# HGRN and modulation in counted steps between the projections, and an earlier load in the FFN

## The chip, the cores and the metric

The kernel runs on one core of a Trainium2 chip. The metric is the device time of one execution in microseconds (us); lower is better. The engines carry the names of the profile: PE (TensorE), DVE (VectorE), ACT (ScalarE), POOL (GpSimd), and SP, which here only issues DMAs. PEld is PE's weight load.

## The reference

One decoder block, sequence 2048, model width 1024, float32. An input projection feeds two mixers, whose outputs are joined by an output projection; a SwiGLU FFN follows.

```
mod = silu(c) @ w_ada + b_ada                     # six vectors of 1024: shift, scale, gate, twice
h   = rms_norm(x, g1) * (1 + scale1) + shift1
hq, hf, hi, hg, aq, ak, av = split(h @ w_in)      # seven slices of 512 columns
# HGRN, 4 heads of 128: gated linear recurrence
state = exp(b_last) * state + (k * exp(b_last - b))^T v
o     = (q * exp(b)) state + (q k^T decayed, causal) v
hgrn  = rms_norm(o) * silu(hg)
# attention, 8 heads of 64: three dilated windows, joined by their softmax denominators
x = x + gate1 * ([hgrn, rms_norm(att)] @ w_out)
h = rms_norm(x, g2) * (1 + scale2) + shift2
x = x + gate2 * ((silu(h @ w_g) * (h @ w_u)) @ w_d)
out = rms_norm(x, final_g)
```

## The kernel before

Products of weights are made in three matmuls: each operand is split into a high and a low part (`whi`, `wlo`, `hhi`, `hlo`), and the product of the two low parts is left out. The sequence lies in four chunks of 512 positions, two to a half. A projection tile is 128x512 in a bank `psA`: eight steps over the model width, three matmuls each (lines 426 to 428 with the weights as columns, 527 to 529 with h). The 28 such tiles of each chunk make 28 x 4 x 24 = 2688 projection matmuls; the text counts the program by them ("the 1253rd").

While they run, the HGRN mixer is computed a head and a chunk at a time (`hg_mix`, 16 units). A unit has preparation (exponentials on ACT, the scan `hb` on DVE), four transposes to `psM` (L576), then seven levels: POOL and ACT make the decay `hd`, DVE makes the operand `hz` (two multiplications), PE makes four 128x128 products in the one bank `psL` (L604), and DVE copies the part under a mask into `hsc` (L609). Then come for each of four blocks the output `psO` (L618, L619), the state's update `psM` (L624) with its read `hst` on DVE (L627, L629), at the end a norm (`ss`, L636) and the store to `hg_d`. float32 matmuls run as two passes, so a level is eight entries of PE in the trace.

The modulation vectors that are needed late (32 of 48 columns of 128) are made in 16 pairs: two weight blocks `adaw` of 512 KB are loaded, DVE multiplies and adds them in eight steps (`adaacc`, L104, L106), two small matmuls sum over partitions (`psM`, L109), and `mods` is written. `x_stats` makes the norm of a chunk (L397), `make_h` the two parts of h (`hhi`, `hlo`).

The program is written in stages (`hg_half`, `token_major`, `att_qk`), and a scheduler moves instructions on every engine by its estimate of when their operands are there. At run time each engine then takes its own queue strictly in that order. Behind the last HGRN units stand the maxima of attention head 0 (L136: products of `qs` and `kh`, loaded back from `qk_d` in DRAM), and `combine` (L150): it transposes the maxima, sends them through DRAM (`m_d`, `mr`), joins the branches (`mm`, `mh`) and writes them back (`mn_d`), from where `qx` takes a row for attention's first scores (L797).

In the FFN's first pass `norm_out` ends the chunk before (sums of squares `ssq`, a matmul `nps` at L297, DVE and ACT apply it), `hr` holds raw blocks of the normalised h, loaded from `h2_d` (L917), and `operand_pieces` splits them into `chi` and `clo` for the first gate and up products `psG` (L904 to L906).

Of the kernel before, what the change touches and what calls it, by code (L numbers as in the profile page):

```python
# [10 lines left out]
F32 = mybir.dt.float32  # L11
# [38 lines left out]
def hybrid_block(ctx, tc, xT, small, cst, w_ada, w_ft, w_tk, w_out, w_gu, w_dn, out):  # L50
# [61 lines left out]

    def ada_pair(pl, pp, cact, g, bufs):
        ps = ada_sums(pl, cact, (g, g + 1), bufs, lambda: pp.tile([P, CH], F32, name="psM", tag="psM", bufs=1))
        tt(dve, mods[:, g:g + 2], ps[:, 0:2], sm[:, V_B + g:V_B + g + 2], ALU.add)
# [204 lines left out]
    def mix_tile(name):  # L320
        return cpool["mr"].tile([P, CH], F32, name="a" + name, tag="a" + name)
# [19 lines left out]
    with ExitStack() as ab:  # L341
# [44 lines left out]
        def x_stats(c, xs=None):  # L386
            ssq = xp.tile([P, CH], F32, name="ssq", tag="ssq", bufs=1)
            for k in range(KT):
                xk = xs[k] if xs else load_xk(c, k)
# [6 lines left out]
            ps = pp.tile([P, CH], F32, name="psM", tag="psM", bufs=1)  # L396
# [23 lines left out]

        def token_major_k(c, k, ps, whi, wlo):
            hhi, hlo = h_of[c]
            cs_ = slice((k % 2) * 512, (k % 2 + 1) * 512)
            for n in range(4):
                ts = slice(n * P, (n + 1) * P)
                pe.matmul(ps[n], hhi[:, k, ts], whi[:, cs_], start=k == 0, stop=False)
                pe.matmul(ps[n], hhi[:, k, ts], wlo[:, cs_], start=False, stop=False)
                pe.matmul(ps[n], hlo[:, k, ts], whi[:, cs_], start=False, stop=k == 7)

        with tc.tile_pool(name="ada0", bufs=2) as pl:  # L430
# [9 lines left out]
            def psum():  # L440
                tag = next(tags)
                return pp.tile([P, CH], F32, name=tag, tag=tag, bufs=1)
# [75 lines left out]
        def feature_major(half, ts, evac):  # L518

            ws_of = [split_w(wp, w_ft[t]) for t in ts]  # L520
            for c, i in [(c, i) for c in (2 * half, 2 * half + 1) for i in range(len(ts))]:
                whi, wlo = ws_of[i]
                hhi, hlo = h_of[c]
                ps = pp.tile([P, CH], F32, name="psA", tag="psA", bufs=4)
                for k in range(KT):
                    ws = slice(k * P, (k + 1) * P)
                    pe.matmul(ps, whi[:, ws], hhi[:, k, :], start=k == 0, stop=False)  # L527
                    pe.matmul(ps, whi[:, ws], hlo[:, k, :], start=False, stop=False)  # L528
                    pe.matmul(ps, wlo[:, ws], hhi[:, k, :], start=False, stop=k == 7)  # L529
                evac(ts[i], c, ps)  # L530

        def att_qk(half, pr):
# [5 lines left out]
            feature_major(half, (12 + pr, 16 + pr), evac)  # L538

        def hg_project(half, hd, js=(0, 1, 2), xs=None):  # L540
            xs = xs or {c: hw.tile([P, 3, CH], F32, name="hx", tag="hx", bufs=3) for c in (2 * half, 2 * half + 1)}

            def evac(t, c, ps):
                dve.tensor_scalar(xs[c][:, t // 4, :], ps, -43.0, None, ALU.max)
# [7 lines left out]
        def hg_mix(hd, c, x):  # L552
# [21 lines left out]
            kt_ps = pp.tile([P, CH], F32, name="psM", tag="psM", bufs=1)  # L574
# [13 lines left out]
            tt(dve, v2(zk)[:, :, 1], v2(kk)[:, :, 1], v2(lr)[:, :, 1], ALU.mult)  # L588
            for lv in range(7):
                h = 1 << lv  # L590
                if lv:
                    zk = zq = T("hz", 2)
                    dd = T("hd", 2)
                    w = lambda t: t.rearrange("p (n two h) -> p n two h", two=2, h=h)
                    ref = w(b)[:, :, 0, h - 1:h].broadcast_to([P, CH // (2 * h), h])
                    tt(pool, w(dd)[:, :, 0, :], ref, w(b)[:, :, 0, :], ALU.subtract)
                    tt(pool, w(dd)[:, :, 1, :], w(b)[:, :, 1, :], ref, ALU.subtract)
                    act.activation(dd, dd, AF.Exp)
                    tt(dve, w(zk)[:, :, 0, :], w(dd)[:, :, 0, :], w(kk)[:, :, 0, :], ALU.mult)
                    tt(dve, w(zk)[:, :, 1, :], w(dd)[:, :, 1, :], w(q)[:, :, 1, :], ALU.mult)  # L600
# [9 lines left out]

            tt(dve, q, q, eb, ALU.mult)
            o_ps = pp.tile([P, CH], F32, name="psO", tag="psO", bufs=1)
            v = v_of[c]
            for n in range(4):
                ts = slice(n * P, (n + 1) * P)
                vn = v[:, n, hd * P:(hd + 1) * P]
                if states[hd] is not None:
                    pe.matmul(o_ps[:, ts], states[hd], q[:, ts], start=n == 0, stop=False, skip_group_check=True)  # L618
                pe.matmul(o_ps[:, ts], vn, sc[:, ts], start=n == 0 and states[hd] is None, stop=n == 3,  # L619
                          skip_group_check=True)  # L620
                if c == NCH - 1 and n == 3:
                    break
                u = pp.tile([P, CH], F32, name="psM", tag="psM", bufs=1)
                pe.matmul(u[:, 0:P], kt[:, ts], vn, start=True, stop=True)  # L624
                new = hw.tile([P, P], F32, name="hst", tag=f"hst{hd}", bufs=2)
                if states[hd] is None:
                    dve.tensor_copy(new, u[:, 0:P])  # L627
                else:
                    dve.scalar_tensor_tensor(new, states[hd], eb[:, n * P + 127:n * P + 128], u[:, 0:P],  # L629
                                             ALU.mult, ALU.add)  # L630
                states[hd] = new
# [3 lines left out]
            ss = pp.tile([P, CH], F32, name="psM", tag="psM", bufs=1)  # L635
# [3 lines left out]
            y = T("hy", 2)  # L639
# [4 lines left out]
        def hg_half(half):  # L644
            first = None
            if half == 0:
                token_major(0, 0, (0,))
                first = hg_project(0, 0, (0, 1))
                token_major(0, 0, (1,))
            else:  # L650
                token_major(half, 0)
            prev = None
            for hd in range(HG_HEADS):
                xs = hg_project(half, hd, (2,), first) if first and hd == 0 else hg_project(half, hd)
                if prev:
                    for c, x in prev[1].items():
                        hg_mix(prev[0], c, x)
                prev = hd, xs
            return prev

        def first_maxima():

            tags = itertools.cycle(("psL", "psO", "psM"))

            def psum():
                tag = next(tags)
                return pp.tile([P, CH], F32, name=tag, tag=tag, bufs=1)
# [3 lines left out]
            for _ in maxima(0, psum):  # L671
                pass
            combine(0, psum)

        for half in range(2):
            if half:
                make_h(2)
            make_h(2 * half + 1)
            last = hg_half(half)
            token_major(half, 1)  # L680
            for pr in range(4):
                att_qk(half, pr)
                if pr == 0:
                    for c, x in last[1].items():
                        hg_mix(last[0], c, x)
                if half and pr == 1:
                    first_maxima()
                if half == 0 and pr == 1:
                    x_stats(2)
                    x_stats(3)  # L690
                if half == 0:
                    for g in range(16 + 8 * pr, 24 + 8 * pr, 2):
                        ada_pair(wp, pp, cact, g, 1)
# [3 lines left out]
    with ax:  # L697
# [135 lines left out]
        def finish_head(hd, c):  # L833
# [4 lines left out]
            rl = ap.tile([64, CH], F32, name="rl", tag="rl", bufs=4)  # L838
# [123 lines left out]
    with ExitStack() as wl, ExitStack() as w0:  # L962
# [3 lines left out]
        for nm in ("hg1", "at1"):  # L966
            c_pool(nm, wl)
# [19 lines left out]
        def norm_out(c, x, ssq, load=False):  # L987
# [36 lines left out]
        for i, (c, j) in enumerate(order):  # L1024
# [32 lines left out]
            if c + 1 < NCH:  # L1057
                if j == 3:
                    xs[c + 1] = load_xw(c + 1)
                if j == 4:  # L1060
# [3 lines left out]
                    last_part = att_half(ats[c + 1], raws, rstd)  # L1064
            if c == NCH - 1:
                if j == 0:
                    wr.close()
                    w0.close()
                    c_pool("hr", wl)
                    c_pool("hp", side="right")  # L1070
                    n = BLK[0][1]
                    tiles = [cpool["hr"].tile([P, KT, T], F32, name="hr", tag=f"hr{b}") for b in range(2)]
                    pieces = operand_pieces(h, [load_block(t, h2_d, b) for b, t in enumerate(tiles)], n,
                                            lambda n: w_tile("hv")[:, 0:n])
# [7 lines left out]
    with cx:  # L1082
# [14 lines left out]
        pace = []  # L1097

        def gate_up(f, h, n, wait=False, first=None):
# [38 lines left out]
            product(p5, parts(b22), h["S4"], start=False)  # L1138
# [66 lines left out]
        for p in range(3):  # L1205
# [103 lines left out]
```

## Time and profile before

| | |
|---|---|
| median of 3 runs | 3038.97 us (3032.05 to 3039.95) |
| profiled execution | 3040.49 us, span 3038.7 us, mean granted clock 0.982 |
| busy | PE 94%, PEld 85%, DVE 68%, POOL 46%, ACT 43% |
| to 107 us | first modulation and norm, first 198 projection matmuls |
| 107 to 978 | the other 2490 projection matmuls, HGRN, late modulation, first maxima |
| 978 to 1362 | attention |
| 1362 to 1575 | output projection |
| 1575 to 1655 | first part of the FFN |
| 1655 to 3039 | the rest of the FFN |

A busy share counts a matmul from its start to its end although the next one starts before that; the distance of starts is what a matmul costs. Idle time of PE is put down to the engine that released it.

### The profile page before, as it was taken

Reading aid. Unit: us, or ns where it says so; the run is one execution under the profiler, and the core shown is the slowest. Engines: PE = TensorE matmul, PEld = TensorE weight load, DVE = VectorE, ACT = ScalarE, POOL = GpSimd, SP = SyncE. Lnnn points to the kernel's source line nnn. Section 1 sums busy time; section 2 is a strip of 40 time slices with the busy share of each in tenths; the row PEclk is TensorE's granted clock in tenths of the full one; section 3 lists DMA queues with packets and bytes.
Section 4 is the critical chain, followed back from the end, with each engine's and each line's share of the span. In section 5 each row is a group of like instructions: output and inputs, shape, how many; then the busy total and the mean of one; then the engine's idle time right before and its main releaser. Section 6 shows DMA issues by size and latency. Waiting matters only on the chain. (4 is left out here: it accounts for less than half of the span.)

```text
span 3038.7 us, 45120 instructions
## 1 busy us (share of the span) xinstructions
PE 2847.3 (94%) x16308; PEld 2592.1 (85%) x16308; DVE 2063.4 (68%) x3781; ACT 1314.0 (43%) x2390; POOL 1411.9 (46%) x1074
## 2 busy tenths in 40 slices
PE   5899998888999999999988999999999999999998
PEld 4777776677778999998768999998999998999997
DVE  7566557667743665677767666679676669776676
ACT  3534423233532566566654333345343335443334
POOL 5344532244532323230035665665666656665664
PEclk9999999999999999999989999999999999999999
DMA  6311237411137756537754222222342223232222
GB/s 239 125 35 36 99 126 236 142 46 35 60 135 188 176 134 140 121 101 244 258 179 155 80 76 64 83 78 91 98 128 81 77 64 106 84 104 74 77 76 68
DMA packets 212031, 343.32 MB, mean 113 GB/s; under 512 B 24784, under 2 KB 97360, under 8 KB 208720
## 3 DMA queue, kind: packets, MB, share of 16 engines
q1 hardware_dynamic: 201984, 322.35, 34.7%
q10 hardware_dynamic: 9824, 18.09, 1.7%
q8 instruction: 128, 2.10, 0.3%
q14 instruction: 95, 0.78, 0.1%
HBM read 281.39 MB, written 58.98 MB: 112 GB/s over the span
## 5 line engine op out<-in xcount | busy, mean ns | idle before, releaser
L79 POOL TENSOR_TENSOR wlo<-wraw,whi 128x512 fp32r<-128x512 f32 (+1 forms) x540 | 845.4, 1586 | 729.5 <-ACT whi L277 384.3
L904 PE MATMUL psG<-chi,whi 128*128 128x344 f32 (+1 forms) x1848 | 597.5, 323 | 20.3 <-DVE hm L79 18.4
L906 PE MATMUL psG<-chi,wlo 128*128 128x344 f32 (+1 forms) x1848 | 593.1, 321 | 2.7 <-POOL wlo L79 2.6
L905 PE MATMUL psG<-clo,whi 128*128 128x344 f32 (+1 forms) x1848 | 594.8, 322 | 0.0
L277 ACT CAST whi<-wraw 128x512 fp32r<-128x512 f32 x520 | 311.7, 618 | 416.6 <-issue 188.8
L904 PEld LDWEIGHTS psG<-chi,whi 128*128 128x128 f32 x1848 | 351.6, 190 | 27.1 <-issue 10.5
L1166 PE MATMUL psD<-ahi,whi 128*128 128x344 f32 (+1 forms) x1056 | 345.5, 327 | 16.3 <-DVE xc L1169 15.8
L906 PEld LDWEIGHTS psG<-chi,wlo 128*128 128x128 f32 x1848 | 350.6, 190 | 3.7 <-POOL wlo L79 3.7
L1169 DVE SCALAR_TENSOR_TENSOR xc<-psD,mods,xc 128x344 f32<-128x344 f32 (+1 forms) x528 | 290.4, 568 | 90.0 <-PE psD L1168 89.7
L905 PEld LDWEIGHTS psG<-clo,whi 128*128 128x128 f32 x1848 | 350.4, 190 | 0.1
L79 POOL TENSOR_TENSOR wlo<-wt,whi 128x512 fp32r<-128x512 f32 x132 | 193.2, 1473 | 313.3 <-ACT whi L277 235.1
L1168 PE MATMUL psD<-ahi,wlo 128*128 128x344 f32 (+1 forms) x1056 | 336.9, 319 | 0.0
L1167 PE MATMUL psD<-alo,whi 128*128 128x344 f32 (+1 forms) x1056 | 335.9, 318 | 0.0
L79 DVE TENSOR_TENSOR hm<-hm,psG 128x344 f32<-128x344 f32 (+1 forms) x330 | 165.9, 503 | 239.3 <-PE psG L906 238.4
L527 PE MATMUL psA<-hhi,whi 128*128 128x512 f32 x640 | 261.1, 409 | 2.6 <-ACT hhi L412 2.6
L528 PE MATMUL psA<-hlo,whi 128*128 128x512 f32 x640 | 259.2, 405 | 0.2 <-DVE hlo L79 0.2
L529 PE MATMUL psA<-hhi,wlo 128*128 128x512 f32 x640 | 258.7, 405 | 0.0
L1166 PEld LDWEIGHTS psD<-ahi,whi 128*128 128x128 f32 x1056 | 198.7, 188 | 32.0 <-DVE xc L1169 27.8
L79 POOL TENSOR_TENSOR hd<-hb 128x256 f32<-128x256 f32 x192 | 134.0, 722 | 164.5 <-DVE hy L640 81.1
L1167 PEld LDWEIGHTS psD<-alo,whi 128*128 128x128 f32 x1056 | 198.8, 188 | 0.5
L1168 PEld LDWEIGHTS psD<-ahi,wlo 128*128 128x128 f32 x1056 | 198.6, 188 | 0.0
L277 ACT CAST whi<-wt 128x512 fp32r<-128x512 f32 x132 | 81.4, 617 | 234.4 <-DVE wt L79 140.1
(239 smaller groups left out, 6030.0 us busy)
## 6 DMA issues: line engine op xcount, KB each, us to landing
wraw<-in_w_gu SPq DMA_DIRECT2D x264, 256.0 KB
wraw<-in_w_dn SPq DMA_DIRECT2D x132, 256.0 KB
adaw<-in_w_ada SPq DMA_DIRECT2D x48, 512.0 KB
wraw<-in_w_ft SPq DMA_DIRECT2D x40, 512.0 KB
wraw<-in_w_tk SPq DMA_DIRECT2D x32, 512.0 KB
qk_d<-st SPq DMA_DIRECT2D x64, 256.0 KB
v<-v_d SPq DMA_DIRECT2D x16, 1024.0 KB
wraw<-in_w_out SPq DMA_DIRECT2D x64, 256.0 KB
```

The lines of the kernel that those rows point to most:

```text
L79: return eng.tensor_tensor(o, a, b, op)
L277: copy(hi, raw)
L527: pe.matmul(ps, whi[:, ws], hhi[:, k, :], start=k == 0, stop=False)
L528: pe.matmul(ps, whi[:, ws], hlo[:, k, :], start=False, stop=False)
L529: pe.matmul(ps, wlo[:, ws], hhi[:, k, :], start=False, stop=k == 7)
L904: pe.matmul(ps, w[0][:, ws], hi, start=start and k == 0, stop=False, skip_group_check=True)
L905: pe.matmul(ps, w[0][:, ws], lo, start=False, stop=False, skip_group_check=True)
L906: last = pe.matmul(ps, w[1][:, ws], hi, start=False, stop=stop and k == 3, skip_group_check=True)
L1166: pe.matmul(ps, w[z][0][:, ws], ahi, start=z == 0, stop=False)
L1167: pe.matmul(ps, w[z][0][:, ws], alo, start=False, stop=False)
L1168: pe.matmul(ps, w[z][1][:, ws], ahi, start=False, stop=z == 1)
L1169: dve.scalar_tensor_tensor(x, ps, ga2[:, j:j + 1], x, ALU.mult, ALU.add)
```

## The change

HGRN's unit, a modulation pair and `x_stats` become Python generators that yield between steps, and PE's order in the projection stage is the order in which the program is written (`manual_schedule`). A class `Beside` is told of every third projection matmul (`tick`) and takes the next step when its count is reached. In the first half two such queues run: the units of the head before, spread over 240 matmuls (its own 144 and the 96 of an attention pair), and the 16 pairs and two norms, spread over 1100. A level's operands are made two levels ahead; the state's four updates stand together ahead of the levels, in one bank, with `psM` in two buffers instead of one. In the second half the third and fourth heads' units are spread over token-major tiles and attention pairs alike. The maxima move from the last tile but one to the last tile's end, and `combine` behind it.

In the FFN the blocks `hr` are loaded a chunk sooner, into a pool of their own, the apply step of `norm_out` works in place, and its last part is released by the end of the first pass's first gate and up product. In attention `rl` has three buffers instead of four.

```diff
+        class Beside:
...
+            def begin(self, work, matmuls, steps, credit=0):
+                self.finish()
+                self.left.extend(work)
+                self.cost, self.credit = matmuls / steps, credit
+            def tick(self, n):
+                self.credit += n
+                while self.left and self.credit >= self.cost:
+                    self.credit -= self.cost
+                    self.step()
...
+            u = pp.tile([P, CH], F32, name="psM", tag="psM", bufs=2)
+            for n in ns:
...
+                pe.matmul(u[:, ts], kt[:, ts], vn[n], start=n == 0, stop=n == ns[-1], skip_group_check=True)
...
             for lv in range(7):
+                yield
+                zk, zq = zs.pop(lv)
...
+                if lv < 5:
+                    level(lv + 2)
...
+        def ada_steps(g):
+            w = wp.tile([P, 2, 8, P], F32, name="adaw", tag="adaw", bufs=1)
...
+            yield
+            yield
...
+            beside_ada.begin([ada_steps(g) for g in range(16, 48, 2)] + [x_stats_steps(2), x_stats_steps(3)],
+                             1100, 16 * 6 + 2 * 6)
+            for hd in range(1, HG_HEADS):
+                beside.begin(units(hd - 1, xs), 240, 2 * UNIT + 1)
+                xs = hg_project(0, hd)
+                att_qk(0, hd - 1)
+            beside.begin(units(3, xs), 288, 2 * UNIT + 1)
...
+            beside.begin(units(3, xs), 192, 2 * UNIT + 1)
+            att_qk(1, 1)
+            att_qk(1, 2)
+            beside.finish()
...
+            beside.begin([maxima(0, psum)], 96 - 36, 24, -36)
+        with tc.manual_schedule(engines={mybir.EngineType.PE}):
+            make_h(1)
+            first_half()
+            make_h(2)
+            make_h(3)
+            second_half()
+            first_maxima()
+            att_qk(1, 3)
+            beside.finish()
+        combine(0, first_psum[0])
...
-                v = w_tile("hv")
-                tt(dve, v, x[:, k, :], rstd, ALU.mult)
+                v = x[:, k, :]
+                tt(dve, v, v, rstd, ALU.mult)
...
+            if (c, j) == (2, 3):
+                blocks = [load_block(cpool["hr"].tile([P, KT, T], F32, name="hr", tag=f"hr{b}"), h2_d, b)
+                          for b in range(2)]
...
-                    steps = norm_out(NCH - 1, xs_last, boxes[NCH - 1]["ssq"], True)
+                    with tc.issue_after(ended[0]):
+                        steps = norm_out(NCH - 1, xs_last, boxes[NCH - 1]["ssq"], True)
```

PE in the first half, at the first HGRN unit, before: `psL` is a level, L624 a state's update, `psA` a projection.

```order
L604 MATMUL psL<-hzq,hz 128x128 x4
L527 MATMUL psA<-hhi,whi 128x512
L624 MATMUL psM<-vtok,hkt 128x128
L528 MATMUL psA<-hlo,whi 128x512
L529 MATMUL psA<-hhi,wlo 128x512
L604 MATMUL psL<-hz 128x128 x4
L624 MATMUL psM<-vtok,hkt 128x128
L527 MATMUL psA<-hhi,whi 128x512
L528 MATMUL psA<-hlo,whi 128x512
L529 MATMUL psA<-hhi,wlo 128x512
L604 MATMUL psL<-hz 128x128 x4
```

The same place now; L657 is the updates' line, L677 the levels', L732 a modulation pair's.

```order
L657 MATMUL psM<-vtok,hkt 128x128 x4
L565 MATMUL psA<-hhi,whi 128x512
L566 MATMUL psA<-hlo,whi 128x512
L567 MATMUL psA<-hhi,wlo 128x512
L732 MATMUL psM<-ones,adaacc 128x1 x2
L565 MATMUL psA<-hhi,whi 128x512
L566 MATMUL psA<-hlo,whi 128x512
L567 MATMUL psA<-hhi,wlo 128x512
L677 MATMUL psL<-hzq,hz 128x128 x4
L565 MATMUL psA<-hhi,whi 128x512
```

Levels stood three to six projection matmuls apart and now stand six to nine apart; the four updates are one group ahead of them, and modulation pairs, which stood between the 1253rd and the 1727th projection matmul for 12 of 16, come about every 60th from the 255th to the 1170th.

PE at the end of the projections before: L136 are the maxima of head 0, L150 is `combine`.

```order
L136 MATMUL psO<-kh,qs 128x128 x2
L136 MATMUL psM<-kh,qs 128x128 x2
L529 MATMUL psA<-hhi,wlo 128x512
L527 MATMUL psA<-hhi,whi 128x512
L528 MATMUL psA<-hlo,whi 128x512
L529 MATMUL psA<-hhi,wlo 128x512
L527 MATMUL psA<-hhi,whi 128x512
L150 MATMUL psL<-idt,mc 128x128
L528 MATMUL psA<-hlo,whi 128x512
L529 MATMUL psA<-hhi,wlo 128x512
```

The same place now; L133 are the maxima (`psS` those of head 1), L147 is `combine`, L896 attention's first scores.

```order
L565 MATMUL psA<-hhi,whi 128x512
L566 MATMUL psA<-hlo,whi 128x512
L567 MATMUL psA<-hhi,wlo 128x512
L133 MATMUL psM<-kh,qs 128x128 x4
L147 MATMUL psL<-idt,mc 128x128
L896 MATMUL psT<-qs,kh 128x256 x3
L133 MATMUL psS<-kh,qs 128x128
L133 MATMUL psS<-kh,qs 128x256 x15
L133 MATMUL psS<-kh,qs 128x128
```

Behind L150 stood 71 projection matmuls. Behind L147 stands none: the last is the row ahead of the last maximum, and head 1's maxima follow.

## Rows read from the trace of the kernel before

**Rows 1.** Busy time by stretch: us, PE, PEld, DVE, ACT, POOL (entries), clock, DMA share, GB/s

```profile
107.00:503.00 396.00, 366.53 (x1859) 291.94 (x1858) 237.43 (x397) 153.52 (x211) 157.00 (x142) 1.00 0.30 100
503.00:614.00 111.00, 95.98 (x398) 75.44 (x397) 77.64 (x120) 36.53 (x43) 31.90 (x14) 0.94 0.51 174
...
1575.00:1655.00 80.00, 59.18 (x322) 54.99 (x323) 60.53 (x76) 40.64 (x72) 58.83 (x40) 0.87 0.49 154
```

**Rows 2.** The same of the whole projection stage

```profile
107.00:978.00 871.00, 799.54 (x3971) 637.84 (x3969) 526.78 (x935) 317.70 (x432) 334.82 (x296) 0.98 0.32 104
```

**Rows 3.** PE's costliest groups, 107 to 978 us: busy, mean ns, idle before and releasers

```profile
L527 PE MATMUL psA<-hhi,whi 128*128 128x512 f32 x608 | 248.3, 408 | 0.0
...
L604 PE MATMUL psL<-hz 128*128 128x128 f32 x768 | 110.0, 287 | 29.1 <-DVE hsc L609 25.4 <-DVE hz L79 3.1
L426 PE MATMUL psA<-whi,hhi 128*128 128x512 f32 x222 | 91.0, 411 | 8.9 <-ACT hhi L412 4.3 <-DVE st L79 3.0 <-DVE hx L544 1.6
...
L109 PE MATMUL psM<-ones,adaacc 128*128 128x1 f32 x64 | 9.2, 248 | 19.2 <-DVE adaacc L106 19.2
```

**Rows 4.** PE in order of time at full clock: start, us, instruction

```profile
229.99 0.39 PE L527 MATMUL psA<-hhi,whi 128*128 128x512 f32 x1
...
230.67 0.39 PE L527 MATMUL psA<-hhi,whi 128*128 128x512 f32 x1
```

**Rows 5.** PE in order of time around four levels: [idle before <-releaser]

```profile
206.81 1.16 PE L604 MATMUL psL<-hz 128*128 128x128 f32 x8
207.72 0.47 PE L528 MATMUL psA<-hlo,whi 128*128 128x512 f32 x1
...
208.74 0.39 PE L529 MATMUL psA<-hhi,wlo 128*128 128x512 f32 x1
211.62 1.16 PE L604 MATMUL psL<-hz 128*128 128x128 f32 x8 [2.49 <-DVE hsc L609]
```

**Rows 6.** DVE's costliest groups, 107 to 978 us

```profile
L79 DVE TENSOR_TENSOR hz<-hd,hk 128x256 f32<-128x256 f32 x96 | 79.4, 827 | 7.4 <-ACT hd L598 6.8
L609 DVE COPY_PREDICATED hsc<-cs,psL 128x512 f32<-128x512 uint32 x96 | 69.7, 726 | 14.9 <-PE psL L604 14.3
L106 DVE SCALAR_TENSOR_TENSOR adaacc<-adaw,cact,adaacc 128x256 f32<-128x256 f32 x101 | 63.7, 631 | 2.3
L79 DVE TENSOR_TENSOR hz<-hd,hq 128x256 f32<-128x256 f32 x96 | 57.3, 597 | 0.0
L544 DVE TENSOR_SCALAR hx<-psA 128x512 f32<-128x512 f32 x45 | 30.9, 687 | 77.5 <-PE psA L529 77.4
```

**Rows 7.** DVE in order of time, the same stretch as rows 5

```profile
206.64 1.81 DVE L79 TENSOR_TENSOR hz<-hd,hk 128x256 f32<-128x256 f32 x1
...
212.27 0.41 DVE L79 TENSOR_TENSOR hz<-hd,hq 128x256 f32<-128x256 f32 x1
```

**Rows 8.** POOL in order of time, the same stretch

```profile
205.60 2.57 POOL L79 TENSOR_TENSOR wlo<-wraw,whi 128x1024 fp32r<-128x1024 f32 x1
```

**Rows 9.** DVE's waits, 450 to 645 us: us in total, times, longest

```profile
DVE adaacc L104 <- DMA adaw<-in_w_ada: 12.2, 7, 4.8
```

**Rows 10.** PE in order of time around the maxima of heads 0 and 1

```profile
943.56 0.39 PE L136 MATMUL psL<-kh,qs 128*128 128x128 f32 x2
...
961.39 0.27 PE L150 MATMUL psL<-idt,mc 128*128 128x128 f32 x1
...
985.56 1.52 PE L136 MATMUL psS<-kh,qs 128*128 128x128 f32 x6 [2.69 <-DMA kh<-qk_d]
```

**Rows 11.** SP's DMA issues around combine

```profile
928.14 0.53 SPq L216 DMA_DIRECT2D qs<-qk_d  x1
...
971.67 0.56 SPq L248 DMA_DIRECT2D qx<-mn_d  x2
```

**Rows 12.** PE's waits, 1575 to 1655 us

```profile
PE nps L297 <- DVE ssq L79: 9.6, 1, 9.6
PE psG L904 <- DVE hm L79: 8.1, 6, 3.9
```

More of the change, by code (lines that the diff above doesn't have):

```diff
@@ L1 @@
 import itertools
+from collections import deque
 from contextlib import ExitStack, nullcontext
@@ L419, in make_h, with __init__, step, finish @@
                 h_apply(c, k)
+        class Beside:
+            def __init__(self):
+                self.left, self.cost, self.credit = deque(), 1, 0
+            def step(self):
+                try:
+                    next(self.left[0])
+                except StopIteration:
+                    self.left.popleft()
+            def begin(self, work, matmuls, steps, credit=0):
[7 more added lines that the diff above has]
+                    self.step()
+            def finish(self):
+                while self.left:
+                    self.step()
+        beside, beside_ada = Beside(), Beside()
+        def tick(n=3):
+            beside.tick(n)
+            beside_ada.tick(n)
         def token_major_k(c, k, ps, whi, wlo):
@@ L516, in token_major, with feature_major @@
                         values_out(ps[n], rows)
-        def feature_major(half, ts, evac):
+        def feature_major(half, ts, evac, chunks=None):
             ws_of = [split_w(wp, w_ft[t]) for t in ts]
-            for c, i in [(c, i) for c in (2 * half, 2 * half + 1) for i in range(len(ts))]:
+            for c, i in [(c, i) for c in chunks or (2 * half, 2 * half + 1) for i in range(len(ts))]:
                 whi, wlo = ws_of[i]
@@ L529, in feature_major, with att_qk @@
                     pe.matmul(ps, wlo[:, ws], hhi[:, k, :], start=False, stop=k == 7)
+                    tick()
                 evac(ts[i], c, ps)
-        def att_qk(half, pr):
+        def att_qk(half, pr, chunks=None):
             def evac(t, c, ps):
@@ L537, in evac @@
                 nc.sync.dma_start(out=qk_d[t - 12][1][:, cc], in_=st_lo)
-            feature_major(half, (12 + pr, 16 + pr), evac)
+            feature_major(half, (12 + pr, 16 + pr), evac, chunks)
         def hg_project(half, hd, js=(0, 1, 2), xs=None):
-            xs = xs or {c: hw.tile([P, 3, CH], F32, name="hx", tag="hx", bufs=3) for c in (2 * half, 2 * half + 1)}
+            xs = {} if xs is None else xs
             def evac(t, c, ps):
+                if c not in xs:
+                    xs[c] = hw.tile([P, 3, CH], F32, name="hx", tag="hx", bufs=3)
                 dve.tensor_scalar(xs[c][:, t // 4, :], ps, -43.0, None, ALU.max)
@@ new lines, in hg_mix @@
+            level(1)
+            yield
+            v = v_of[c]
+            vn = [v[:, n, hd * P:(hd + 1) * P] for n in range(4)]
+            ns = range(3 if c == NCH - 1 else 4)
+            u = pp.tile([P, CH], F32, name="psM", tag="psM", bufs=2)
+            for n in ns:
+                ts = slice(n * P, (n + 1) * P)
+                pe.matmul(u[:, ts], kt[:, ts], vn[n], start=n == 0, stop=n == ns[-1], skip_group_check=True)
+            before = [states[hd]]
+            for n in ns:
+                ts = slice(n * P, (n + 1) * P)
+                new = hw.tile([P, P], F32, name="hst", tag=f"hst{hd}", bufs=2) if n == 3 else \
+                    hw.tile([P, P], F32, name="hst", tag="hst", bufs=3)
+                if before[-1] is None:
+                    dve.tensor_copy(new, u[:, ts])
+                else:
+                    dve.scalar_tensor_tensor(new, before[-1], eb[:, n * P + 127:n * P + 128], u[:, ts],
+                                             ALU.mult, ALU.add)
+                before.append(new)
@@ L642, in hg_mix @@
             nc.sync.dma_start(out=hg_d[hd][c], in_=y)
[L644 to L659, printed above, removed]
+        UNIT = 16
@@ new lines, in units @@
+        def units(hd, xs):
+            return [hg_mix(hd, c, x) for c, x in xs.items()]
+        def ada_steps(g):
+            w = wp.tile([P, 2, 8, P], F32, name="adaw", tag="adaw", bufs=1)
+            for j in range(2):
+                nc.sync.dma_start(out=w[:, j].rearrange("p k c -> p (k c)"), in_=w_ada[g + j])
+            yield
+            yield
+            acc = wp.tile([P, 2, P], F32, name="adaacc", tag="adaacc", bufs=2)
+            for k in range(8):
+                if k == 0:
+                    dve.tensor_scalar(acc, w[:, :, k, :], cact[:, k:k + 1], None, ALU.mult)
+                else:
+                    dve.scalar_tensor_tensor(acc, w[:, :, k, :], cact[:, k:k + 1], acc, ALU.mult, ALU.add)
+                if k == 3:
+                    yield
+            yield
+            yield
+            ps = pp.tile([P, CH], F32, name="psM", tag="psM", bufs=2)
+            for j in range(2):
+                pe.matmul(ps[:, j:j + 1], acc[:, j, :], ones[:, 0:1], start=j == 0, stop=j == 1,
+                          skip_group_check=True)
+            tt(dve, mods[:, g:g + 2], ps[:, 0:2], sm[:, V_B + g:V_B + g + 2], ALU.add)
@@ new lines, in second_half @@
+        def second_half():
+            token_major(1, 0)
+            xs = hg_project(1, 0)
+            for hd, others in ((1, lambda: att_qk(1, 0)), (2, lambda: token_major(1, 1, (2,))),
+                               (3, lambda: token_major(1, 1, (3,)))):
+                beside.begin(units(hd - 1, xs), 240, 2 * UNIT + 1)
+                xs = hg_project(1, hd)
+                others()
+            beside.begin(units(3, xs), 192, 2 * UNIT + 1)
+            att_qk(1, 1)
+            att_qk(1, 2)
+            beside.finish()
@@ L673, in first_maxima @@
[L673 to L693, printed above, removed]
+            beside.begin([maxima(0, psum)], 96 - 36, 24, -36)
@@ L1068, in hybrid_block @@
                     w0.close()
-                    c_pool("hr", wl)
                     c_pool("hp", side="right")
                     n = BLK[0][1]
-                    tiles = [cpool["hr"].tile([P, KT, T], F32, name="hr", tag=f"hr{b}") for b in range(2)]
-                    pieces = operand_pieces(h, [load_block(t, h2_d, b) for b, t in enumerate(tiles)], n,
-                                            lambda n: w_tile("hv")[:, 0:n])
+                    pieces = operand_pieces(h, blocks, n, lambda n: w_tile("hv")[:, 0:n])
                 else:
@@ L1137, in gate_up @@
             silu[:] = [act.activation(e[1], e[1], AF.Silu).ins]
-            product(p5, parts(b22), h["S4"], start=False)
+            ended[:] = [product(p5, parts(b22), h["S4"], start=False)]
             tt(dve, e[0], e[0], p5, ALU.add)
```

99 lines of the change are left out of this document (55 added, 44 removed).

## The prediction

> **What bounds the kernel now.** I read the busy shares first: PE 94%, DVE 68%, POOL 46%, so PE sets the length of most stretches. The slices by time and the table by stretch say where it does not: the projection stage, 107 to 978 us, has PE busy for 799.54 of 871 us at a mean clock of 0.98 [rows 2], while attention and the FFN behind 1655 us are nearly full. So I work out what PE would need in that stage if it never waited, by the distance of starts and not by busy time.
>
> A projection matmul starts (230.67 - 229.99) / 3 = 0.227 us after the one before it at full clock [rows 4]. The stage has 3 x 608 + 3 x 222 = 2490 of them [rows 3], 565 us. An HGRN level of eight entries takes 207.72 - 206.81 = 0.91 us [rows 5], 0.114 an entry. By the code a unit has seven levels (6.4 us), 28 entries for transposes, updates and outputs (3.2) and a norm of two wide passes (0.45): 10.0 us, and 16 units 160 us. Some 9 us are left for modulation, norms and maxima (64, 4 and 48 entries at 0.06 to 0.23). The floor is 734 us, and the stage loses 871 - 734 = 137 us.
>
> Where it goes: idle time that the trace names is 871 - 799.5 = 71.5 us, most of it at the levels (29.1, of which 25.4 for `hsc`) and at the modulation pairs (19.2 for `adaacc`) [rows 3]. A level is released by DVE's read of the level before. That read and the two `hz` cost 0.726 + 0.827 + 0.597 = 2.15 us of DVE [rows 6], and PE has only three to six projection matmuls (0.7 to 1.4 us) and 0.91 us of its own between two levels. With five between, PE still stood 2.49 us [rows 5], since the scan and a long `hz` lay on DVE. The clock's 0.98 stands for 871 x 0.02 = 17 us. The rest is the array running empty behind each wait: from 208.74 to 211.62 are 2.88 us, so the cost is 2.65 where 2.49 is named [rows 5], and many gaps too short to be named.
>
> **The projection stage after.** The matmuls, POOL's and DVE's operations stay the same in kind and number, so the floor of 734 us stays; only the 137 us can change.
>
> *First half.* Between two levels now lie on average 7.27 projection matmuls (240 in 33 steps), 1.65 us, plus 0.91: 2.56 us of PE against 2.15 of DVE. But DVE also takes the modulation: 16 pairs x 8 operations x 0.631 [rows 6] = 81 us, over 1100 matmuls and the eight units' PE time (1100 x 0.227 + 7 x 10 = 320 us), 0.65 us a step; and the projections' evacuations, 0.687 each [rows 6], one per 24 matmuls, 0.21 a step or somewhat more where an attention tile takes two. That is 3.0 us gross in a step of 2.56; consecutive DVE operations overlap by about 0.08 us in the trace (five a step), so 2.6 net. DVE is about even with PE in the seven level steps of a unit and has less to do in the other nine. I take 0.1 to 0.6 us a level over 56 levels (6 to 34 us) and choose 16 us; with waits for the weight blocks `adaw` and the weights' low parts 6 us more. `adaw` has one buffer, its next load waits for the eight steps of the last, and the row of today's crowded stretch has 12.2 us for seven, at most 4.8 [rows 9]; a step's wait now has two yields in front, some 20 matmuls or 4.6 us. So 22 us are left.
>
> *The chunks of h between the halves.* This stretch of 111 us runs at 0.94 (111 x 0.06 = 6.7 us) [rows 1], and the waits for `adaacc` lie mostly here. They go with the pairs. What is late next is h itself: 4.3 us for `hhi` [rows 3]. I leave 6.
>
> *Second half.* No modulation; a step has 2.56 us of PE (six matmuls for the last head, 2.27) against 2.15 to 2.4 of DVE. I leave 11 us, 1.4 a unit, for the state's chain, which now has four DVE operations in a row between its group and the output, and 5 us for the evacuations that wait in [rows 3] and stay.
>
> *Maxima.* Their operands are loaded back from DRAM behind the stores of the 2592nd matmul's tile. Before, the first maximum ran at 943.56, 15.4 us after the first load's issue at 928.14 [rows 10, 11]. Now the first maximum stands 39 matmuls (8.9 us) behind that tile, so PE stands at it; the bounds are 0 (the loads are in time by fewer bytes) and 15 us. I take 9, and 2 for the clock behind it. The stage thus keeps 22 + 6 + 16 + 11 = 55 of 137 us: 82 us gained.
>
> *The chain of `combine`.* Before, it ran from its transpose at 961.39 to the last load at 971.67 and some 2 us of landing [rows 10, 11], 13 us, beside 71 projection matmuls (16 us): hidden. Now what stands behind it is three score matmuls and head 1's maxima, whose operands can be there (about 40 entries, at most 5 us). A wait is added at the first use of `qx`, and attention's whole PE queue is behind it. Cost 8 to 17 us with the slow clock after such an idle time; I take 17 less the 5 us that head 1's maxima cost today (a wait of 2.69 us for `kh` [rows 10] and their slow start): 12 us lost.
>
> **The FFN's start.** From 1575 to 1655 us PE waits 9.6 us for the norm's `ssq`, because DVE is busy with the blocks, and 8.1 us for `hm`; the clock is 0.87, another 80 x 0.13 = 10 us [rows 12, 1]. With `hr` loaded a chunk sooner its splitting can start ahead, and the norm's last part stands behind the first gate and up product, so the 9.6 us go and part of the slow clock with them. DVE's and POOL's work is the same, so `hm`'s waits stay. Gain 5 to 20 us, I take 13. The in-place step removes a buffer, not an operation; its work lies on DVE ahead of PE's backlog: 0, at worst 2. `rl` with three buffers: 0 by the full PE of attention, at worst 3.
>
> **Sum.** -82 + 12 - 13 = -83 us on the profiled execution's 3040.5 is 2957.5; the median lies 1.5 lower: 2956.
>
> A rule speaks against spreading. An `hz` of 0.41 us when POOL is idle took 1.81 us beside POOL's `wlo` (205.60 to 208.17) [rows 7, 8]. The Trainium skill (SBUF — State Buffer, "Who interferes with whom") says that a VectorE instruction with two SBUF inputs and a GpSimd one that reads SBUF share a port under an exclusive lock, and that the later one is blocked for the whole instruction; the trace agrees, 1.40 us beside 0.41. The work of both engines stays while the stage gets 9% shorter, so by this rule more of it would meet: the part of `hz` over 0.41 is now (0.827 + 0.597 - 0.82) x 96 = 58 us [rows 6], and 9% more is 5 us of DVE. The sum would be 2961 where DVE sets the end, 2956 where not.
>
> **The rivals.**
> *A. DVE becomes the bound of the units.* For it: 3.0 us gross against 2.56 in the first half, and long `hz`. Against it: DVE is busy for only 237 of 396 us there [rows 1]. Then 0.45 us a level more over the first half's 56 (25 us), and 0.2 over the second's (11): 2956 + 36 = 2992.
> *B. PE's fixed order costs more than it saves; slower.* Before, the scheduler put a late operand's matmul behind others that were ready; now its place is fixed by a count. A unit has about 11 such places (transposes, updates, seven levels, output, norm), 176 in all, and modulation, norms and maxima add 40. If each waits 83 / 216 = 0.38 us more than I left, the gain is gone; it decides from 0.43 us on, where 0.3% is passed. Waits like the 2.49 us [rows 5] or the 4.8 us [rows 9] at every fifth place would do it. At 0.5 us: 2956 + 108 = 3064. Against it: levels stand further apart, not nearer.
> *C. The earlier load does nothing*, because DVE and POOL, not the load, are late at the FFN's start: the 13 us stay, 2969.
> *D. PE nearly reaches its floor*: 30 us of waits fewer and 5 more at the FFN's start: 2921.
>
> **How the numbers follow.** The forecast, with its own range of 2935 to 2980, has 0.44; A 0.20, C 0.10, D 0.14, B 0.08; 0.04 is left for a time within 0.3% of before (9 us), about what a measurement of this kernel tells from no change, the three runs lying 0.26% apart. The range cuts B and the ends of A and D: 2918 to 3000. Faster 0.88, the same 0.04, slower 0.08.
>
> **What would show it.** Right: the span between the 198th and the last projection matmul falls from 871 to about 790 us; waits of levels for `hsc` fall below 15 us and those of the pairs for `adaacc` below 4; a new PE wait of 5 to 12 us for `kh` at the first maximum and one of 8 to 15 us at the first use of `qx` or just ahead; no wait for `ssq` at the FFN's start. Wrong: level waits for `hz` or `hsc` of 0.5 us at most levels of the first half (A), waits spread over updates, transposes and outputs too (B), or `hm` and `clo` late by as much as `ssq` was (C).

## The result: 1.07% faster, where 2.7% was forecast

| | before | after |
|---|---|---|
| median | 3039.46 us (3032.05 to 3043.17, 4 runs) | 3006.56 us (3002.39 to 3007.76, 4 runs) |
| ratio | | 0.9893, 95% interval 0.9880 to 0.9906 |
| profiled run: span, clock | 3038.7, 0.982 | 3004.2, 0.979 |
| behind the 198th to the last projection matmul | 106.7 to 977.4: 871 us | 102.0 to 939.3: 837 us |
| from there to attention's first output product | 4.5 | 28.4 |
| end of attention (its last product) | 1386.8 | 1359.1 |
| first gate or up matmul of the FFN | 1572.9 | 1547.9 |
| 432 gate and up matmuls later | 1687.4 | 1652.2 |

Attention before thus ends at 1386.8, where the table of stretches above has 1362. By these marks before less after is 4.7 us behind the 198th projection matmul, 38.1 at the last, 27.7 at attention's end, 25.0 when the FFN starts and 35.2 some way into it. So the projections gave 33 us and the stretch to the 198th another 5; the new seam between projections and attention took 10 and the output projection 3; the FFN's start gave 10.

The projection stage by the stretch view (us; busy PE, PEld, DVE, ACT, POOL; clock; DMA), which answers to [rows 2]:

```profile
102.00:939.00 837.00, 775.23 (x3961) 644.10 (x3960) 505.90 (x914) 318.50 (x433) 335.70 (x296) 0.98 0.33 109
```

PE's floor there was put at 734 us, so 103 of the 137 us that were lost still are, where 55 were forecast. Counted as in the prediction they are 62 us of named idle time (837 - 775.23; 71.5 before), 17 of clock (17) and 24 in gaps too short to be named (48): what was won lies mostly in the short gaps. PE's waits after the change, in the second half (580 to 899 us: us in total, times, longest), where no modulation runs:

```profile
PE psM L657 <- ACT hkt L622: 10.0, 5, 3.6
PE psL L677 <- DVE hsc L682: 9.0, 7, 2.2
```

and in the first half (102 to 491 us):

```profile
PE psL L677 <- DVE hsc L682: 14.1, 13, 2.0
PE psM L657 <- ACT hkt L622: 8.8, 5, 2.5
```

The waits for `adaacc` of [rows 3] (19.2 us) are gone, and level waits for `hsc` (25.4 before) are 23.1. The 18.8 us for `hkt`, ACT's copy of the four transposes, are new: the state's updates stand six or nine projection matmuls (1.4 or 2 us) behind the transposes, since the count is looked at only at every third matmul and its mean step of 7.27 comes out as six or nine. All eight units with six wait, 16.8 us in all; of the eight with nine two do. What they wait for is read from ACT, in order of time (start, us, instruction):

```profile
699.91 1.47 ACT L597 ACTIVATE he<-hx 128x1536 f32<-128x1536 f32 x1
...
701.91 1.47 ACT L598 ACTIVATE he<-he 128x1536 f32<-128x1536 f32 x1
703.42 1.48 ACT L599 ACTIVATE he<-he 128x1536 f32<-128x1536 f32 x1
704.80 0.57 ACT L622 COPY hkt<-psM 128x512 f32<-128x512 f32 x1
```

The transposes start on PE at 701.45. The three `he` belong to the next unit; the scheduler put them ahead of this unit's copy, and PE stood until the copy was there. In seven of the ten waits (14.2 us) these exponentials stand directly ahead of the copy. PE, at the same place:

```profile
701.45 0.60 PE L620 MATMUL psM<-cs,hkd 128*128 128x128 f32 x4
...
705.42 0.94 PE L657 MATMUL psM<-vtok,hkt 128*128 128x128 f32 x6 [1.98 <-ACT hkt L622]
...
722.07 1.16 PE L677 MATMUL psL<-hz 128*128 128x128 f32 x8 [2.23 <-DVE hsc L682]
```

The longest wait for `hkt`, 3.60 us at 872.07, is in the last unit, which has no next one. There a decay `hd` of the unit itself stands ahead of the copy and idles for POOL:

```profile
870.91 0.63 ACT L644 ACTIVATE hd<-hd 128x512 f32<-128x512 f32 x1 [3.85 <-POOL hd L80]
871.45 0.57 ACT L622 COPY hkt<-psM 128x512 f32<-128x512 f32 x1
```

The row at 722.07 is a level's wait. Its reason is on DVE:

```profile
716.16 2.38 DVE L80 TENSOR_TENSOR hz<-hd,hk 128x256 f32<-128x256 f32 x1
718.46 0.41 DVE L80 TENSOR_TENSOR hz<-hd,hq 128x256 f32<-128x256 f32 x1
720.17 1.22 DVE L607 TENSOR_TENSOR_SCAN hb<-rst,hlf 128x512 f32<-128x512 f32 x1 [1.30 <-POOL hd L80]
721.32 0.70 DVE L682 COPY_PREDICATED hsc<-cs,psL 128x512 f32<-128x512 uint32 x1
```

and on POOL:

```profile
715.86 2.39 POOL L80 TENSOR_TENSOR wlo<-wraw,whi 128x1024 fp32r<-128x1024 f32 x1
718.95 1.19 POOL L80 TENSOR_TENSOR hd<-hb 128x256 f32<-128x256 f32 x2 [0.70 <-DVE hz L80]
```

The scan is the next unit's. It stands ahead of this unit's read `hsc`, idles 1.30 us until POOL has made this unit's last `hd` out of the one buffer `hb`, and then runs for 1.22, while the read that PE waits for is behind it. So DVE stands idle just before PE has to wait for it. A scan stands directly ahead of the read in six of the second half's seven level waits. In the first half that is so in four of 13, and three of the five longest have four operations of a modulation pair in the scan's place, as ahead of the read that a level at 160 us waited for:

```profile
156.17 2.91 DVE L725 SCALAR_TENSOR_TENSOR adaacc<-adaw,cact,adaacc 128x256 f32<-128x256 f32 x4
159.00 0.72 DVE L682 COPY_PREDICATED hsc<-cs,psL 128x512 f32<-128x512 uint32 x1
```

At the seam, PE, which answers to [rows 10]:

```profile
916.14 0.77 PE L133 MATMUL psL<-kh,qs 128*128 128x128 f32 x2 [8.13 <-DMA kh<-qk_d]
...
941.08 0.30 PE L147 MATMUL psL<-idt,mc 128*128 128x128 f32 x1 [0.66 <-issue]
941.14 0.60 PE L896 MATMUL psT<-qs,kh 128*128 128x256 f32 x3
947.91 1.62 PE L133 MATMUL psS<-kh,qs 128*128 128x128 f32 x6 [6.18 <-DMA mr<-m_d]
...
963.57 0.51 PE L898 MATMUL psT<-qx,kl 128*128 128x256 f32 x1
```

and SP's issues, to [rows 11]:

```profile
903.16 0.53 SPq L213 DMA_DIRECT2D qs<-qk_d  x1
...
953.21 0.64 SPq L245 DMA_DIRECT2D qx<-mn_d  x2
```

The first maximum waits 8.1 us for its operands, 13 us behind the issue of the first load. From `combine`'s transpose at 941.08 to the first use of `qx` are 22.5 us, of which head 1's maxima fill about 16; the mean clock from 939 to 963 us is 0.63, so most of that stretch ran at the lower of its two levels (1.2 and 2.4 GHz), with the idle 6 us in it. The profile puts the 6.18 us down to `mr`, which head 1's maxima do not read; in six other runs here it names their `kh` at this place.

The FFN's start, to [rows 12]: `nps` is no longer waited for, `hm` costs 3.1 instead of 8.1 us, and two waits of another kind are new, for a weight and for the first `psD`.

```profile
PE psG L1003 <- ACT whi L274: 6.2, 1, 6.2
PE psD L1265 <- DVE xc L1268: 3.2, 1, 3.2
PE psG L1003 <- DVE hm L80: 3.1, 3, 1.5
```

### The profile page after: what moved, and what is told of

It reads as the page before. It is cut to its first block, busy times and chain, and to the rows that moved or that the text cites. A ratio compares the mean times of both kernels' runs of the same rounds, so it can differ in the third digit from the quotient of the medians.

```text
span 3004.2 us, 45023 instructions
## 1 busy us (share of the span) xinstructions
PE 2829.4 (94%) x16308; PEld 2601.9 (87%) x16308; DVE 2041.7 (68%) x3781; ACT 1313.2 (44%) x2392; POOL 1404.8 (47%) x1076
## 5 line engine op out<-in xcount | busy, mean ns | idle before, releaser
L1003 PE MATMUL psG<-chi,whi 128*128 128x344 f32 (+1 forms) x1848 | 596.4, 323 | 20.8 <-DVE hm L80 14.1
L565 PE MATMUL psA<-hhi,whi 128*128 128x512 f32 x640 | 272.1, 425 | 4.3 <-ACT hhi L417 2.6
L566 PE MATMUL psA<-hlo,whi 128*128 128x512 f32 x640 | 253.0, 395 | 0.6 <-DVE hlo L80 0.6
```

Of the source, the lines that this page charges most:

```text
L1003: pe.matmul(ps, w[0][:, ws], hi, start=start and k == 0, stop=False, skip_group_check=True)
```

## Experiments

Medians are of several runs; ratios are to the kernel before on the same chip, which ran 3034.6 to 3038.0 us. The changed kernel has 0.9893, so 0.0033 of ratio are 10 us. Gains below are the difference of the two ratios.

| kernel | median, us | ratio (95%) |
|---|---|---|
| FFN part alone | 3024.0 | 0.9967 (0.9954 to 0.9980) |
| updates behind the third level | 2992.5 | 0.9853 (0.9837 to 0.9870) |
| two buffers for `hb` | 2991.5 | 0.9853 (0.9838 to 0.9868) |
| less modulation | 2992.5 | 0.9855 (0.9840 to 0.9870) |
| two orders by hand | 2998.3 | 0.9870 (0.9855 to 0.9884) |
| earlier maxima | 3009.0 | 0.9903 (0.9887 to 0.9920) |
| PE's order free | 2990.2 | 0.9843 (0.9827 to 0.9858) |
| `wlo` in pieces | 3010.5 | 0.9910 (0.9895 to 0.9926) |
| free, `hb`, updates | 2977.1 | 0.9812 (0.9783 to 0.9840) |
| other end, pinned | 2978.3 | 0.9812 (0.9790 to 0.9835) |
| other end, free | 2975.4 | 0.9805 (0.9785 to 0.9826) |
| free, `hb`, updates, steps of two | 2971.7 | 0.9791 (0.9770 to 0.9812) |

**FFN part alone**: the kernel before with the diff's lines from attention on.

> The kernel before with the FFN part of the change alone (raw blocks a chunk sooner, apply in place, last part behind the first gate and up product). Theory: the start of the FFN is worth about 10 us by itself, as the start of one part to the start of the next in the two traces shows (35.2 - 25.0): 3027 to 3031 us, and no wait of the norm's matmul for ssq there. Rival: the gain there hangs on the projection stage's earlier end, or is taken back later: 3036 to 3040 us.

3024.0 against 3034.6: 10.6 us, a little beyond the range. The gain is the FFN's own.

**Updates behind the third level.**

```diff
-            u = pp.tile(...)            # ahead of the levels
...
+                if lv == 2:
+                    u = pp.tile(...)    # and the four updates and reads, unchanged
```

> The changed kernel with the four state updates of a unit moved from ahead of the first level to behind the third. Theory (a fixed place on PE meets an operand that ACT makes late, because ACT's own queue has the next unit's three exponentials of 1.48 us ahead of the copy hkt): the 18.8 us of waits for hkt go and come back nowhere, 2986 to 2992 us. Rival (DVE has no room, so any wait removed turns up at the next level): waits for hsc grow by as much, 3002 to 3008 us.

12 us gained, the slow end of the theory's range. The waits for `hkt` are gone, but level waits rose from 23.1 to 32.3 us, so half came back, which is the rival's part:

```profile
PE psL L658 <- DVE hsc L663: 28.8, 24, 2.8
...
PE psL L658 <- DVE hsc L80: 3.5, 3, 1.8
```

**Two buffers for `hb`.**

```diff
-            ... T("hlf"), T("hb"), T("heb")
+            ... T("hlf"), T("hb", 2), T("heb")
...
-            kt = T("hkt")
+            kt = kd
```

> The changed kernel with two buffers for the scan's result hb (room made by writing the copy of the transposes over their source). Theory (the next unit's scan stands on DVE ahead of a level's read and waits 1.3 us for POOL to end with the old hb): each of the long level waits in the second half shrinks by about 1.3 us, some 9 us there and 3 in the first half, 2993 to 2998 us. Rival (DVE's throughput bounds the levels): the waits for hsc stay near 23 us, 3004 to 3008 us.

12 us gained, and the level waits of the second half fell from 9.0 us to a single one of 1.7; the six behind a scan are gone. The wait for the transposes' copy stays (18.5 us). What the scan waited for did cost a level each time.

**Less modulation**: seven of eight multiply-adds of each pair are left out.

> The changed kernel without seven of the eight multiply-adds of each modulation pair (the loads, the first product and the small matmuls stay), which leaves part of the modulation out. Theory (queue order): the level waits with three or four of these operations in a row ahead of the read go (about 8 of 14 us for hsc in the first half), those behind a scan stay, and the second half does not change: 2994 to 3000 us. Rival (DVE is the bound of the first half): all level waits of the first half go and the stretch shortens by more, 16 us or more: under 2991 us.

11.5 us gained. In the first half `hsc` fell from 14.1 to 8.8 us and did not go; seven of the nine waits that are left there have the next unit's scan directly ahead of the read. In the second half it stayed at 9.1 (9.0). The queue's order fits better than throughput, and leaving out some 70 us of DVE's work (16 x 7 x 0.631 [rows 6]) was worth no more than one buffer.

**Two orders by hand.**

```diff
+            with tc.issue_after(last_kt[0]) if last_kt else nullcontext():
                 act.activation(e, x, AF.Exp, scale=-1.0)
...
+            with tc.issue_after(last_read[0]) if last_read else nullcontext():
                 dve.tensor_tensor_scan(b, rst, lf, 0.0, ALU.mult, ALU.add)
```

> The changed kernel with two orders set by hand and nothing else: on ACT the next unit's three exponentials stand behind this unit's copy hkt, on DVE the next unit's scan and its two neighbours stand behind this unit's last level read. Theory (the order in ACT's and DVE's queues is what PE waits for): waits for hkt fall from 18.8 to under 4 us, and level waits in the second half from 9 to under 3; both gains add up, 2976 to 2984 us, as far below the changed kernel as the two single edits together. Rival (throughput: a wait removed turns up at another step, as nearly half did when the updates were moved): 2988 to 2998 us, with new waits at the transposes, since the preparation starts later.

Only 7 us, at the rival's slow end. `hkt` fell to 3.9 and levels to 13.6 us, as the theory has it, but a new wait stands at the unit's norm, because ACT now has the later preparation (L620) ahead of the square that the norm needs (L707), in all seven cases:

```profile
PE psL L684 <- DVE hsc L689: 13.6, 11, 2.2
PE psM L710 <- ACT hd L707: 12.4, 7, 2.1
```

```profile
616.24 0.63 ACT L620 ACTIVATE hkd<-hkd 128x512 f32<-128x512 f32 x1 [0.85 <-POOL hkd L80]
616.78 0.58 ACT L707 ACTIVATE hd<-psO 128x512 f32<-128x512 f32 x1
```

So an order is what PE waits for, but a better one isn't had by pushing one chain back as a whole.

**Earlier maxima.**

```diff
-            beside.begin(units(3, xs), 192, 2 * UNIT + 1)
+            beside.begin(units(3, xs), 144, 2 * UNIT + 1)
...
-            att_qk(1, 2)
+            att_qk(1, 2, (2,))
```

> The changed kernel with the last head's units spread over 144 instead of 192 projection matmuls, so that the first maxima end 48 matmuls (11 us) ahead of the last projection. Theory (the way of the maxima through DRAM, from the last maximum to qx, is what attention waits for): the 24 us between the last projection and the first qx shrink by about 10; the wait for kh at the first maximum stays; 2995 to 2999 us. Rival (denser units cost as much: 4.4 matmuls a step, 1.9 us of PE against 2.15 of DVE over 14 levels): 3001 to 3006 us.

No gain (the interval takes in the changed kernel's). The seam shrank from 28.4 to 18.9 us as expected, but level waits rose from 23.1 to 28.3 and the last projection came 13 us later: the rival, somewhat stronger than priced.

**PE's order free.**

```diff
-        with tc.manual_schedule(engines={mybir.EngineType.PE}):
+        with nullcontext():
```

> The changed kernel with PE's order in the projection stage left to the scheduler; the program is written in the same steps. Theory (the text's order and the other engines' queues decide, not the pinning): within 4 us of the changed kernel, 3002 to 3010 us. Rival (a fixed order on PE makes every late operand a wait): 2985 to 2998 us with it freed.

15 us gained: the theory fell. The units' waits are as in the changed kernel (25.2 us for `hsc`, 16.7 for `hkt`), so the rival's reason did not hold for them. Their order is nearly the same too, with single matmuls exchanged; the scheduler moved the first maxima behind most of the last tile's matmuls. Most of the gain lies there: the 2592nd projection matmul runs at 893.2 (899.0), the last at 917.3 (939.3), and attention's first output product comes at 951.9 instead of 967.7, so that 10 of these 16 us lie behind the 2592nd. The 8.1 us for `kh` are gone from PE's projections. For the 6 us ahead of it no wait is named, and no run here tells why:

```profile
912.25 0.39 PE L133 MATMUL psL<-kh,qs 128*128 128x128 f32 x2
...
937.75 9.57 PE L133 MATMUL psS<-kh,qs 128*128 128x128 f32 x29 [9.20 <-DMA kh<-qk_d]
```

**`wlo` in pieces.**

```diff
-        tt(lo_eng or pool, lo, raw, hi.bitcast(F32), ALU.subtract)
+        for z in range(4):
+            tt(lo_eng or pool, lo[:, zs], raw[:, zs], hi[:, zs].bitcast(F32), ALU.subtract)
```

> The changed kernel with POOL's low parts of the projections' weights made in four pieces of 256 columns instead of one of 1024. Theory (an hz beside one such operation is held up to 2.4 us and delays the level's read): the long hz fall to about 1 us, and with them 4 to 8 us of level waits go: 2998 to 3003 us. Rival (the reads are late by the order of the queues, whatever hz takes): within 3 us of the changed kernel, or slower by POOL's extra starts, 3004 to 3012 us.

No gain; level waits were 25.2 us. The edit did what it should: the longest `hz` fell from 2.61 to 0.96 us. But POOL took 213 us for these low parts instead of 162, and the scan of the next unit, which idled 1.30 us for POOL at this place, now idled longer:

```profile
724.89 1.22 DVE L609 TENSOR_TENSOR_SCAN hb<-rst,hlf 128x512 f32<-128x512 f32 x1 [2.47 <-POOL hd L80]
```

So this run does not tell what the long `hz` alone cost.

**Three edits together**: free order, two `hb`, updates behind the first level.

> Three edits together on the changed kernel: PE's order left to the scheduler, two buffers for hb, the four state updates behind the first level instead of ahead of it. Theory (three separate waits: for the maxima's operands at the end, for the scan's buffer, for the copy hkt): the gains add up, about 15 + 12 us and 8 to 12 of the 17 to 19 for hkt, 2968 to 2975 us. Rival (each edit frees the same time, since DVE has no more room): 2982 to 2990 us, as the best of them alone.

25 us below the changed kernel, just beyond the theory's slow end and between the two. The 18.8 us for the copy are down to 1.3. What is left is the scan again: with a buffer of its own it stands ahead of the first level's read instead of the fourth's, and takes 2.63 us there instead of 1.22. It then runs beside POOL's `wlo`: the six scans of this run that start beside one take 2.63 to 2.65 us, and where POOL is idle they take 1.21 to 1.23.

```profile
622.42 2.63 DVE L607 TENSOR_TENSOR_SCAN hb<-rst,hlf 128x512 f32<-128x512 f32 x1 [0.70 <-ACT hlf L606]
624.97 0.66 DVE L80 TENSOR_TENSOR hsc<-psL,cs 128x512 f32<-128x512 f32 x1
```

```profile
621.58 2.39 POOL L80 TENSOR_TENSOR wlo<-wraw,whi 128x1024 fp32r<-128x1024 f32 x1
```

**Another end of the stage, pinned and free**: second-half units over 192 matmuls, the last head's over 240, 192 projections behind them, `combine` as a step ahead of the last 42.

> The changed kernel with two hb buffers, updates behind the first level, PE's order still pinned, and another end of the projection stage: units of the second half over 192 instead of 240 matmuls, the last head's over 240, 192 projection matmuls behind them, of which 72 pass before the first maximum and 42 behind combine. Theory (it is not the pinning but the place that was chosen: the maxima stood 39 matmuls behind a load that takes 16 us, and nothing behind combine): no wait for kh at the first maximum, 14 to 20 us less between the last projection and attention's first output than the 28 us of the changed kernel, 2962 to 2975 us. Rival (denser units take it back: 5.8 matmuls a step, 2.2 us of PE against 2.15 to 2.4 of DVE, over 42 levels): waits for hsc in the second half over 10 us and 2978 to 2992 us.

> The same as the one before (two hb buffers, later updates, the other end of the stage), with PE's order left to the scheduler. Theory (with the places right, pinning costs nothing): within 5 us of it. Rival (the scheduler's few swaps are worth something of their own): 8 to 15 us faster than it.

Both as fast as the three edits, not faster, 3 us beyond the theory's range and at the rival's edge. Pinned or free makes no difference that can be told (2978.3 and 2975.4). So pinning costs nothing by itself once other places are pinned; that its 15 us hung on the maxima's place is the best reading, with the 6 us ahead of them left over. The wait for `kh` is gone (0.17 us) and the seam is 15.1 us, but level waits are back at 32.1 us, 13.5 of them in the second half (7.3 with the three edits): both the theory's gain and the rival's price are there.

**Steps of two.**

```diff
-                if k == 3:
+                if k in (1, 3, 5):
```

> Three edits (free order, two hb buffers, later updates) and the modulation's multiply-adds in steps of two instead of four. Theory (in the first half it is the run of four such operations, 2.5 to 2.9 us, ahead of a level's read): 3 to 6 us below the kernel without this edit. Rival (DVE's throughput): the same within 2 us.

The fastest kernel, 0.9791, 31 us below the changed one; against the same without this edit the intervals overlap, so this edit's share (5 us) is not shown. Level waits of 25.0 us remain (25.4 without it); three of the longer ones in the first half have a scan of 2.6 us ahead of the read.

## Why the prediction was wrong

The direction and the size at the seam and the FFN were right. The wait for `kh` at the first maximum is there (8.1 us, forecast 9). Attention's end shows 10.4 us lost at the seam (12 forecast), but its parts are others: PE idled 6 us ahead of head 1's maxima where 8 to 15 were put at or ahead of `qx`, and these maxima filled 16 us where at most 5 were counted. That the sum comes out is in part luck. The FFN's start gave 10.2 us in the traces and 10.6 alone (13 forecast). The chunks of h between the halves and the waits of the modulation pairs went as said.

The step that failed is what the units keep: "So 22 us are left" in the first half and "I leave 11 us, 1.4 a unit, for the state's chain" with 5 for evacuations in the second. The first took 389.6 us (102.0 to 491.6) for 1146 projection matmuls, eight units and the small matmuls, whose starts need 346, and the second 319 (580 to 899) for 882, where they need 280: they keep 43 and 39, against 22 and 16. Both terms were sums of durations: DVE's work in a step against PE's, on average, and an engine that is even with PE in a sum was taken to be in time. The 16 us put on the first half's levels did come out in size (14.1), but mostly for another reason, which is luck. The runs show two things in the place of that sum, and the traces a third.

First, a term was missing. The updates now stand ahead of the levels, and no price was set on the copy `hkt` on ACT that they need. It cost 18.8 us in waits, most of them (14.2) with the next unit's 4.4 us of exponentials directly ahead of it; moving the updates removed the wait and gained 12 us. Rival B named such places, but at all of them; it was at one of them, in ten of 16 units.

Second, the levels' waits are set mostly by what stands ahead of the read in DVE's queue, less by DVE's load. Two buffers for `hb` gave 12 us without taking any work away, and in the second half, where the sum had 2.15 to 2.4 us of DVE against 2.56 of PE, one level in six of eight units waited for the next unit's scan. Rival A had the place (levels) and the wrong reason (throughput): without most of the modulation, 8.8 of the first half's 14.1 us of level waits stayed.

Third, the clock was counted among today's 137 us (17 for the stage) and then left out of what the halves keep:

```profile
102.00:491.00 389.00, 362.78 (x1893) 300.90 (x1892) 267.81 (x474) 155.96 (x213) 165.31 (x144) 0.99 0.36 126
580.00:899.00 319.00, 295.94 (x1564) 246.88 (x1563) 188.50 (x306) 123.85 (x173) 132.39 (x133) 0.97 0.20 73
```

By the prediction's own way of counting that is 389 x 0.01 + 319 x 0.03, some 14 us. With the named waits (26 and 23 us) 63 of the 82 us are accounted for; the other 19 lie in gaps too short to be named, and no run here takes them apart.

The expected lengthening of `hz` beside POOL's `wlo` is there (2.38 us at 716.16), and the scan shows it too when it starts beside one (2.63 us). But pieces of `wlo` gained nothing and cost POOL more, so no time of the whole is shown to hang on it alone.

Not priced at all was the 4.7 us up to the 198th projection matmul; all other runs here have it within some 2 us (100.6 to 104.1). The FFN part alone is among them (102.9), and its projections are those of the kernel before, so the steps are not needed for it; no run here tells what is. Where the rest of the first half's level waits come from when steps are halved also stays open.

## What to carry to other kernels

When a change spaces work out by a count, check for each place not the sum of durations but the queue of the engine that makes the operand: what stands ahead of it there, and what that in turn waits for. Look also at the shortest step that the count gives (six matmuls here), not only at its mean (7.27). Pinning one engine's order does not pin the engines that feed it; a scheduler that pulls the next unit's start forward puts it ahead of the reads that the pinned engine needs. A buffer that lets the pulled-forward work pass can be worth as much as removing a good part of the work.

## What was not expected

Leaving PE's order to the scheduler was worth 15 us, though the one named wait that went with it was 8.1 us. And a wait removed came back in part in several of the runs, most plainly at the unit's norm (12.4 us) when both queues were set by hand.
